# A Strassen-form MLP down projection with its matmul operands exchanged, on one core

## The chip, the core and the metric

The kernel runs on one core of one Trainium2 chip. TensorE (PE) multiplies: a stationary operand of 128x128 is loaded (PEld), then columns of a moving operand stream past it and accumulate in PSUM. VectorE (DVE) and ScalarE (ACT) work element by element, GpSimd (POOL) issues a few DMAs here, and SyncE (SP) issues most of them. The metric is the device time of one execution in microseconds, lower is better.

## The reference, cut to what matters

One layer: an input projection into two recurrent mixers, an output projection, cross attention, an MLP with squared ReLU, and a last RMSNorm. There are 512 tokens, a model width D of 2048 and a hidden width of 8192, all float32.

```python
h += concat[GDN(y_gdn), RWKV7(y_rwkv)] @ W_out
h += CrossAttn(RMSNorm(h), RMSNorm(mem))
h += SquaredReLU-MLP(RMSNorm(h))      # up: (512 x 2048) @ (2048 x 8192), square(relu), down: @ (8192 x 2048)
out = RMSNorm_final(h)
```

## The kernel before

Every product is taken in float32 precision out of float32r pieces: split() (lines 128 to 135) makes a rounded hi of a tile on ScalarE and the rest lo on VectorE, and TensorE accumulates hi·hi, hi·lo and lo·hi. Weights come through a ring of raw tiles ("ua", three buffers, and "ub", four; raw(), line 1435, loads issued by SP) and are split into rings of two ("whi", "wlo").

Up and down are each done by a Strassen form with seven products over 2x2 blocks instead of eight. In up, strassen(p) makes the hidden activations in 32 steps p of 20.16 us: seven products B11, T1, T2, B21, T3, B22, T4 (in p = 0 B21 comes second) of 24 matmuls each, with sums of weight blocks on VectorE, then the combinations of the outputs that down needs, stored to DRAM (Cd) through ScalarE's DMA queue. The product T1 of p = 0 is followed by the norm of the MLP's input: a matmul "pss", then rsq() (two ScalarE operations, lines 125 and 126), whose result is first used after product B22.

Down has four blocks c of the hidden width (2048 each). piece_() loads one combination of Cd (through SP) and splits it into activation tiles "dh" and "dl"; the list todo holds the pieces in order, and later(n) makes the next n. In a block there are seven products: 0 (weight block A11), 1 (A12), then a middle loop with 2 (S1), 3 (S1 + A11) and 4 (that + A12), then 5 (S3) and 6 (A22). The sums S1 and S3 of weight blocks are formed ahead of time by POOL: a DMA writes a block to DRAM (SUMS, "ws") and a second one adds another block to it; 18 such pairs are issued in the output projection, and 14 more by ticks in up (odd p). Each call of down() takes 1024 rows of weights by 128 output features: block() splits the tile and runs 16 matmuls with hi and 8 with lo, weights stationary, 256 tokens moving. Two calls share a PSUM bank of 128 features x 2x256 tokens, and into() adds a finished bank to the residual "hq", which lies by features (partition = feature). In the last block final() squares the results, norm() sums the squares over partitions with a matmul of ones ("pss"), and scaled() multiplies by gain and norm and stores the output by features; the half HB is finished during product 6, the half HA at the very end.

From the input projection to its end a planner in the kernel writes the order out by hand. From the output projection on, including up and down, the framework's scheduler orders each engine's instructions by their place in the program and by when it expects their data; each queue then runs in that fixed order. The tiles' semaphores follow from the data.

Of the kernel before, what the change touches and what calls it, by code (L numbers as in the profile page):

```python
# [9 lines left out]
F32 = mybir.dt.float32  # L10
# [26 lines left out]
for _n, _w in (("norm_mix", 16), ("norm_xattn", 16), ("norm_mem", 16), ("norm_mlp", 16),  # L37
               ("norm_final", 16), ("mu", 27), ("w0", 8), ("a0", 8), ("kk", 8), ("ka", 8),
               ("rk", 8), ("lnw", 8), ("lnb", 8), ("conv", 96), ("gnw", 1), ("dtb", 1),
               ("alog", 1)):  # L40
    PRM[_n] = (_off, _w)
    _off += _w
# [31 lines left out]
def build(tc, I, out):  # L74
# [268 lines left out]

    SUMS = {i: [pd.tile([P, 2048], F32, name=f"ws{i}_{u}", tag=f"ws{i}_{u}") for u in range(16)] for i in (0, 1)}
    Cd = [pd.tile([P, 7, 512], F32, name=f"cd{q}", tag=f"cd{q}") for q in range(16)]
# [953 lines left out]
    tock = pc.tile([P, 1], F32, name="tock")  # L1299
    wanted = [(i, c * 4 + u) for c in range(4) for i in (0, 1) for u in range(4)]  # L1300

    def background(h, n):

        tc.keep_in_program_order(GP.tensor_copy(tock, h[:, 0:1]))
        for _ in range(n):
            i, u = wanted.pop(0)
            tc.keep_in_program_order(GP.dma_start(SUMS[i][u], I["w_dn"][u, (2, 0)[i]]))
            tc.keep_in_program_order(GP.dma_start(SUMS[i][u], I["w_dn"][u, 1], accum_op=ALU.add, max_dma_last_dim=2048))

# [10 lines left out]
    for n in range(KD):  # L1320
        xr = sl2()
        nc.sync.dma_start(xr, I["xT"][:, n, :])
        pt = psb(f"op{n}", "mm", 2)
        gemm(pt, I["w_out"][n], KD, oh, ol)
        V.tensor_tensor(out=hres[n], in0=pt, in1=xr, op=ALU.add)
        hi, lo = act_tile(f"hh{n}"), act_tile(f"hl{n}")
        split(hres[n], hi, lo, col("norm_xattn", n))
        hh_.append(hi)
        hl_.append(lo)
        finish(n, acc)  # L1330
        if n == 0:
            background(hres[n], 18)
    pcol = psb("pcol")
# [76 lines left out]
    def add(o, a, b):  # L1410
        V.tensor_tensor(out=o, in0=a, in1=b, op=ALU.add)
# [38 lines left out]
    def strassen(p, done, used):  # L1450
# [46 lines left out]
        sub(t4, c2[:, HA], t[:, HB])  # L1497
        if p % 2 and p > 1 and wanted:
            S.copy(ticks[:, p:p + 1], c2[:, 0:1])
            background(ticks[:, p:p + 1], 1)  # L1500
# [47 lines left out]

    todo = []

    for p in range(32):
# [4 lines left out]
        def used(i):  # L1556
            if p == 0 and i == T1:
                pt = psb("pss2", "scr", 1)
                mm(pt, ones, acc)
                rsq(rstd, pt, 1.0 / 2048, b_eps6)  # L1560
            if p == 31 and i in (T1, T2, T3):
                for q in ((0,), (1, 2), (3,))[i - T1]:
                    piece_(0, 0, q)

        strassen(p, square, used)

    def later(n):
# [3 lines left out]

    EV, OD = 0, 1
    view = lambda t: t.rearrange("p (a b) -> p a b", b=M)

    def into(a, par, half, pt, op):
        h = hq[a][par][:, :, half]
        V.tensor_tensor(out=h, in0=h, in1=view(pt), op=op)

    def weights(c, m, b):
        u = c * 4 + m // 2  # L1580
        src = SUMS[b - 4][u] if b >= 4 else I["w_dn"][u, b]
        return src[:, m % 2 * 1024:m % 2 * 1024 + 1024]

    A11, A21, A22, A12, S1, S3 = range(6)

    def down(c, i, m, pt, a, start):
        parts = []
        for k in range(8):
            hi, lo = had[c, i][k // 2]
            s_ = slice(k % 2 * M, k % 2 * M + M)  # L1590
            parts.append((hi[:, s_], lo[:, s_]))
        block(pt[:, m % 2 * M:m % 2 * M + M], a, parts, start and m % 2 == 0)

    TAGS = (("mg", 2), ("mg", 2), ("scr", 1), ("scg", 1))
    sums = {}

    def final(a, par, half):

        sq = sl2()
        S.activation(view(sq), hq[a][par][:, :, half], AF.Square)  # L1600
        nm = "A" if half is HA else "B"
        if nm not in sums:
            sums[nm] = (ph if half is HB else pu).tile([P, T], F32, tag="acc" if half is HB else "ur", name=f"fs{nm}", bufs=1)
            V.tensor_copy(sums[nm], sq)
        elif (a, par, nm) == (3, OD, "A"):
            sums["last"] = sq
        else:
            add(sums[nm], sums[nm], sq)

    def norm(half, parts):  # L1610
        pt = psb("pss3", "mg")[:, HA]
        parts = [x[:, y] for x in parts for y in (HA, HB)]
        for j, x in enumerate(parts):
            mm(pt, ones, x, start=j == 0, stop=j == len(parts) - 1)
        rsq(rstd[:, half], pt, 1.0 / 2048, b_eps6)

    def scaled(n, half):
        h = hres[n][:, half]
        V.scalar_tensor_tensor(out=h, in0=h, scalar=col("norm_final", n), in1=rstd[:, half],
                               op0=ALU.mult, op1=ALU.mult)  # L1620
        (nc.sync if n % 2 else nc.scalar).dma_start(out[n][:, half], h)

    todo += [(0, i, q) for i in range(1, 7) for q in range(4)]
    SUB, ADD = ALU.subtract, ALU.add
    for c in range(4):
        end = c == 3
        nx = lambda *l: [(c + 1, i, q) for i in l for q in range(4)] if not end else []
        X = [psb(f"dx{c}_{a}", ("mx", "mm")[a // 2]) for a in range(4)]
        for m in range(8):
            down(c, 0, m, X[m // 2], raw(weights(c, m, A11)), True)  # L1630
            if m % 2:
                into(m // 2, EV, HA, X[m // 2], SUB)
            later(1)
        todo += nx(0)
        for m in range(8):
            if m % 2 == 0:
                z = psb(f"dz{c}_{m}", *TAGS[m // 2])
            down(c, 1, m, z, raw(weights(c, m, A12)), True)
            if m % 2:
                into(m // 2, EV, HA, z, ADD)  # L1640
                if end:
                    final(m // 2, EV, HA)
            later(1)
        todo += nx(1)
        for a in range(4):
            y = psb(f"dy{c}_{a}", *TAGS[a])
            ms = (2 * a, 2 * a + 1)
            s1 = [raw(weights(c, m, S1)) for m in ms]
            for m in ms:
                down(c, 2, m, y, s1[m % 2], True)  # L1650
            into(a, OD, HB, y, ADD)
            a11 = [raw(weights(c, m, A11)) for m in ms]
            for m in ms:
                add(s1[m % 2], s1[m % 2], a11[m % 2])
                down(c, 3, m, X[a], s1[m % 2], False)
            into(a, EV, HB, X[a], SUB)
            a12 = [raw(weights(c, m, A12)) for m in ms]
            for m in ms:
                add(a12[m % 2], a12[m % 2], s1[m % 2])
                down(c, 4, m, y, a12[m % 2], False)  # L1660
            into(a, EV, HB, y, SUB)
            if end:
                final(a, EV, HB)
            later(2 if c == 0 else 1)
        todo += nx(2, 3, 4)
        for m in range(8):
            down(c, 5, m, X[m // 2], raw(weights(c, m, S3)), False)
            if m % 2:
                into(m // 2, OD, HB, X[m // 2], ADD)
                if end:  # L1670
                    final(m // 2, OD, HB)
            later(1)
        todo += nx(5)
        for m in range(8):
            down(c, 6, m, X[m // 2], raw(weights(c, m, A22)), False)
            if m % 2:
                into(m // 2, OD, HA, X[m // 2], ADD)
                if end:
                    final(m // 2, OD, HA)
            later(1)  # L1680
            if end and m == 0:
                norm(HB, [sums["B"]])
                S.activation(rcol[:, 0:1], rstd[:, HB][:, 0:1], AF.Ln)
            elif end:
                for n in range((m - 1) * 16 // 7, m * 16 // 7):
                    scaled(n, HB)
        todo += nx(6)
    norm(HA, [sums["A"], sums["last"]])
    for n in range(KD):
        scaled(n, HA)  # L1690
    pu_cm.__exit__(None, None, None)
# [3 lines left out]
def layout(inputs):  # L1695
# [33 lines left out]
    for n in ("norm_mix", "norm_xattn", "norm_mem", "norm_mlp"):  # L1729
        put(n, cols(a[n][0]))  # L1730
    put("norm_final", cols(a["norm_final"]))
    mu = a["rwkv_mu"][0]
# [37 lines left out]
    d["w_up"] = blocks7(a["mlp_w_up"][0])  # L1770
    wd = blocks7(a["mlp_w_down"][0]).reshape(4, 2, 4, P, 4, 1024)
    d["w_dn"] = np.ascontiguousarray(wd.transpose(4, 0, 2, 3, 1, 5).reshape(16, 4, P, 2048))
    return d
# [16 lines left out]
```

## Time and profile before

| | |
|---|---|
| median of 3 runs | 3021.33 us (3020.08 to 3025.76) |
| the profiled execution | 3018.6 us, span 3016.8 us |
| TensorE, weight loads | busy 99% and 89% of the span |
| VectorE, ScalarE, POOL | 69%, 49%, 9% |
| chain that ended last | 92% TensorE |
| stages on TensorE | output projection from 1331, attention from 1505, up from about 1689, down from 2348 to 3002 |

Times in the profile are microseconds from the start of the span. A row of a group gives the line, the engine, the operation, the output and inputs with their shapes, how many there were, the sum of their times and the mean in ns, and the idle time before them. Matmuls overlap each other, so the spacing of their starts, not their mean length, is what a stream of them costs. A row of the order of time gives the start, the length and the number of instructions merged.

### The profile page before, as it was taken

Reading aid. Unit: us, or ns where it says so; the run is one execution under the profiler, and the core shown is the slowest. Engines: PE = TensorE matmul, PEld = TensorE weight load, DVE = VectorE, ACT = ScalarE, POOL = GpSimd, SP = SyncE. Lnnn points to the kernel's source line nnn. Section 1 sums busy time; section 2 is a strip of 40 time slices with the busy share of each in tenths; the row PEclk is TensorE's granted clock in tenths of the full one; section 3 lists DMA queues with packets and bytes.
Section 4 is the critical chain, followed back from the end, with each engine's and each line's share of the span. In section 5 each row is a group of like instructions: output and inputs, shape, how many; then the busy total and the mean of one; then the engine's idle time right before and its main releaser. Section 6 shows DMA issues by size and latency. Waiting matters only on the chain.

```text
span 3016.8 us, 56151 instructions
## 1 busy us (share of the span) xinstructions
PE 2972.4 (99%) x22912; PEld 2672.2 (89%) x22912; DVE 2077.9 (69%) x2925; ACT 1484.6 (49%) x2014; POOL 271.8 (9%) x626
## 2 busy tenths in 40 slices
PE   9999999999999999999999999999999999999998
PEld 7788878878877898878887899999999999999998
DVE  7666666666677646544437788888887886868676
ACT  6454545544556555543325544444444544444444
POOL 0302212213213000001110000000000000000000
PEclk9999999999999999999999999999999999999999
DMA  5323423323425487789994367677677877676654
GB/s 185 102 88 81 108 72 90 101 81 89 129 70 161 149 267 244 247 260 273 261 237 128 119 187 200 194 204 199 196 206 207 274 248 233 214 251 203 235 182 154
DMA packets 284626, 537.70 MB, mean 178 GB/s; under 512 B 95752, under 2 KB 148236, under 8 KB 283856
## 3 DMA queue, kind: packets, MB, share of 16 engines
q1 hardware_dynamic: 228816, 427.15, 45.7%
q0 software_dynamic: 17920, 67.11, 9.8%
q10 hardware_dynamic: 37632, 39.86, 3.7%
q8 instruction: 179, 2.93, 0.4%
q14 instruction: 79, 0.65, 0.1%
HBM read 473.86 MB, written 127.28 MB: 199 GB/s over the span
## 4 chain that ended last, share of the span: by engine, by line
PE 92%; DMA 2%; DVE 2%; ACT 2%; issue 1%; POOL 0%; ACTq 0%; SPq 0%; DVEq 0%; POOLq 0%
PE py L247 21%; PE upx L1445 8%; PE dx L1445 7%; PE op L122 6%; PE dx L1448 4%; PE upy L1445 4%; PE upx L1448 4%; PE dy L1445 4%; PE kq L247 3%; PE vo L122 3%; PE vp L122 3%; PE sc L122 3%; PE at L122 3%; PE kp L247 2%; PE dz L1445 2%; PE upy L1448 2%
## 5 line engine op out<-in xcount | busy, mean ns | idle before, releaser
L130 ACT CAST whi<-ub 128x1024 fp32r<-128x1024 f32 x259 | 271.1, 1048 | 289.5 <-PE dx L1445 73.7
L131 DVE TENSOR_TENSOR wlo<-ub,whi 128x1024 fp32r<-128x1024 f32 x259 | 316.1, 1221 | 90.9 <-ACT whi L130 90.3
L247 PE MATMUL py<-xhi,whi 128*128 128x512 f32 x928 | 371.5, 400 | 6.6 <-ACT xhi L247 6.6
L247 PE MATMUL py<-xhi,wlo 128*128 128x512 f32 x928 | 371.9, 401 | 0.0
L247 PE MATMUL py<-xlo,whi 128*128 128x512 f32 x928 | 371.4, 400 | 0.0
L247 DVE TENSOR_TENSOR wlo<-wraw,whi 128x1024 fp32r<-128x1024 f32 (+1 forms) x180 | 223.4, 1241 | 128.1 <-ACT whi L247 124.2
L130 ACT CAST whi<-ua 128x1024 fp32r<-128x1024 f32 x189 | 198.0, 1048 | 213.0 <-PE dx L1445 54.4
L247 ACT CAST whi<-wraw 128x1024 fp32r<-128x1024 f32 (+1 forms) x180 | 188.1, 1045 | 203.3 <-PE py L247 162.0
L1445 PE MATMUL upx<-cb,whi 128*128 128x256 f32 x2048 | 268.6, 284 | 4.8 <-ACT whi L130 4.5
L131 DVE TENSOR_TENSOR wlo<-ua,whi 128x1024 fp32r<-128x1024 f32 x189 | 230.7, 1221 | 58.3 <-ACT whi L130 56.5
L1445 PEld LDWEIGHTS upx<-cb,whi 128*128 128x128 f32 x2048 | 256.5, 193 | 5.7 <-ACT whi L130 5.4
L1445 PE MATMUL dx<-dh,whi 128*128 128x256 f32 x1024 | 252.1, 284 | 4.3 <-ACT whi L130 4.3
L1445 PE MATMUL dx<-dl,whi 128*128 128x256 f32 x1024 | 251.2, 283 | 0.0
L131 DVE TENSOR_TENSOR wlo<-wraw,whi 128x1024 fp32r<-128x1024 f32 x112 | 137.2, 1225 | 114.3 <-ACT whi L130 112.8
L247 PEld LDWEIGHTS py<-xhi,whi 128*128 128x128 f32 x928 | 175.0, 189 | 41.0 <-ACT xhi L247 6.6
L247 PEld LDWEIGHTS py<-xhi,wlo 128*128 128x128 f32 x928 | 175.0, 189 | 35.2 <-issue 1.0
L247 PEld LDWEIGHTS py<-xlo,whi 128*128 128x128 f32 x928 | 174.9, 188 | 35.0 <-DVE xlo L247 0.7
L1445 PEld LDWEIGHTS dx<-dh,whi 128*128 128x128 f32 x1024 | 196.5, 192 | 5.7 <-ACT whi L130 5.7
L1445 PEld LDWEIGHTS dx<-dl,whi 128*128 128x128 f32 x1024 | 196.5, 192 | 0.0
L130 ACT CAST whi<-wraw 128x1024 fp32r<-128x1024 f32 x112 | 117.8, 1052 | 155.9 <-PE op L122 68.9
L1448 PE MATMUL upx<-cb,wlo 128*128 128x256 f32 x1024 | 144.1, 283 | 0.0
L1448 PE MATMUL dx<-dh,wlo 128*128 128x256 f32 x1024 | 143.8, 283 | 0.1
(784 smaller groups left out, 6973.3 us busy)
## 6 DMA issues: line engine op xcount, KB each, us to landing
wraw<-in_w_in SPq DMA_DIRECT2D x116, 512.0 KB, 3.9
ub<-in_w_dn SPq DMA_DIRECT2D x88, 512.0 KB, 4.8
ua<-in_w_dn SPq DMA_DIRECT2D x72, 512.0 KB, 4.5
ub<-in_w_up SPq DMA_DIRECT2D x71, 512.0 KB, 4.7
ws<-in_w_dn POOLq DMA_DIRECT2D x32, 1024.0 KB, 11.9
ua<-in_w_up SPq DMA_DIRECT2D x57, 512.0 KB, 5.2
sl<-cd SPq DMA_DIRECT2D x104, 256.0 KB, 4.7
ub<-ws SPq DMA_DIRECT2D x40, 512.0 KB, 4.6
```

Of the source, the lines that this page charges most:

```text
L122: PE.matmul(o, l, r, start=start, stop=stop)
L130: S.copy(hi, src)
L131: V.tensor_tensor(out=lo, in0=src, in1=hi.bitcast(F32), op=ALU.subtract)
L247: f(*a, **k)
L1445: PE.matmul(pt, hi[:, k * P:k * P + P], x, start=start, stop=False, skip_group_check=True)
L1448: PE.matmul(pt, lo[:, k * P:k * P + P], parts[k][0], start=False, stop=k == 7, skip_group_check=True)
```

## The change

In down(), the operands change places. A call now takes 256 rows of the contraction (one piece q) by 512 output features: the activations are stationary, 128 tokens at a time, and 512 weight columns move. A call runs 12 matmuls instead of 24, and there are as many calls. Results lie by tokens, so the residual is needed by tokens too: turn() transposes it on TensorE in up (p = 2 to 17) and stores it to DRAM (HTd), held() loads it back into the same SBUF as "G" (p = 20 to 27). The squares of the last norm are summed along the row by ScalarE (accum_out), the gain is loaded as four broadcast rows, and the output is stored by tokens. The weights are laid out anew on the host. SUMS has 64 tiles of half the size, 36 pairs in the output projection and one at each p from 2 to 29. The norm of up follows T3 instead of T1. The middle loop holds four s1 tiles (in "ub") and goes through products 2, 3 and 4 with four calls each, for two halves m of the output.

```diff
-    wanted = [(i, c * 4 + u) for c in range(4) for i in (0, 1) for u in range(4)]
+    wanted = [(i, c * 8 + u) for c in range(4) for i in (0, 1) for u in range(8)]
...
-            background(hres[n], 18)
+            background(hres[n], 36)
...
-        if p % 2 and p > 1 and wanted:
+        if p > 1 and wanted:
             S.copy(ticks[:, p:p + 1], c2[:, 0:1])
             background(ticks[:, p:p + 1], 1)
...
+    def turn(a, t):
+        pt = psb(f"ht{a}_{t}", ("scr", "scg")[t % 2], 1)
+        for j in range(4):
+            PE.transpose(pt[:, j * P:(j + 1) * P], hres[4 * a + j][:, t * P:(t + 1) * P], ident)
+        r = (ph if t % 2 else pu).tile([P, T], F32, tag=("ur", "acc")[t % 2], name=f"hr{a}_{t}", bufs=1)
+        S.copy(r, pt)
+        nc.sync.dma_start(HTd[:, t, a * 512:a * 512 + 512], r)
+
+    def held(t, m):
+        i = t * 2 + m
+        G[t][m] = ph.tile([P, 2, T], F32, tag=f"h{i // 2}{i % 2}", name=f"g{t}{m}", bufs=1)
+        nc.sync.dma_start(G[t][m], HTd[:, t, m * 1024:m * 1024 + 1024].rearrange("p (a b) -> p a b", b=T))
...
-            if p == 0 and i == T1:
+            if p == 0 and i == T3:
                 pt = psb("pss2", "scr", 1)
                 mm(pt, ones, acc)
                 rsq(rstd, pt, 1.0 / 2048, b_eps6)
...
         strassen(p, square, used)
+        if 2 <= p < 18:
+            turn((p - 2) // 4, (p - 2) % 4)
+        elif 20 <= p < 28:
+            held((p - 20) // 2, p % 2)
...
+    def into(half, blk, m, pts, op):
+        for t in (0, 1):
+            g = G[2 * half + t][m][:, blk, :]
+            V.tensor_tensor(out=g, in0=g, in1=pts[t], op=op)
...
+    def down(c, i, q, pts, a, start):
+        cnt[0] += 1
+        hi = pw.tile([P, 1024], F32R, tag="whi", name=f"whi{cnt[0]}", bufs=NWS)
+        lo = pw.tile([P, 1024], F32R, tag="wlo", name=f"wlo{cnt[0]}", bufs=NWS)
+        split(a, hi, lo)
+        uh, ul = had[c, i][q]
+        st = [(z, t, slice(z * M + t * P, z * M + t * P + P), slice(z * 512, z * 512 + 512)) for z in (0, 1) for t in (0, 1)]
+        for z, t, x, w in st:
+            PE.matmul(pts[t], uh[:, x], hi[:, w], start=start and z == 0 and q == 0, stop=False, skip_group_check=True)
+            PE.matmul(pts[t], ul[:, x], hi[:, w], start=False, stop=False, skip_group_check=True)
+        for z, t, x, w in st:
+            PE.matmul(pts[t], uh[:, x], lo[:, w], start=False, stop=z == 1 and q == 3, skip_group_check=True)
...
+    def final(half, blk, m):
+        for t in (2 * half, 2 * half + 1):
+            i = t * 4 + m * 2 + blk
+            S.activation(sl2(), G[t][m][:, blk, :], AF.Square, accum_out=ss[:, i:i + 1])
+
+    def norm(half):
+        h = slice(2 * half, 2 * half + 2)
+        V.tensor_reduce(out=rt[:, h], in_=ss[:, half * 8:half * 8 + 8].rearrange("p (a b) -> p a b", b=4), axis=AX.X, op=ALU.add)
+        rsq(rt[:, h], rt[:, h], 1.0 / 2048, b_eps6)
+
+    def scaled(t, n):
+        g = G[t][n // 2][:, n % 2, :]
+        V.scalar_tensor_tensor(out=g, in0=g, scalar=rt[:, t:t + 1], in1=gain[n], op0=ALU.mult, op1=ALU.mult)
+        (nc.sync if n % 2 else nc.scalar).dma_start(out[t][:, n * 512:n * 512 + 512], g)
...
+        for m in (0, 1):
+            y = [psb(f"dy{c}_{m}{t}", *TAGS[m][t]) for t in (0, 1)]
+            s1 = []
+            for q in range(4):
+                u = (c * 2 + m) * 4 + q
+                s1.append(raw(SUMS[0][u], 0))
+                down(c, 2, q, y, s1[q], True)
+            into(1, 1, m, y, ADD)
+            for q in range(4):
+                a = raw(I["w_dn"][(c * 2 + m) * 4 + q, A11], 1)
+                add(s1[q], s1[q], a)
+                down(c, 3, q, X[m], s1[q], False)
+            into(1, 0, m, X[m], SUB)
+            for q in range(4):
+                a = raw(I["w_dn"][(c * 2 + m) * 4 + q, A12], 1)
+                add(a, a, s1[q])
+                down(c, 4, q, y, a, False)
+                if c == 0 and q % 2:
+                    later(1)
+            into(1, 0, m, y, SUB)
...
+    norm(0)
+    for n in range(4):
+        for t in (0, 1):
+            scaled(t, n)
```

More of the change, by code (lines that the diff above doesn't have):

```diff
@@ L37 @@
 for _n, _w in (("norm_mix", 16), ("norm_xattn", 16), ("norm_mem", 16), ("norm_mlp", 16),
-               ("norm_final", 16), ("mu", 27), ("w0", 8), ("a0", 8), ("kk", 8), ("ka", 8),
+               ("mu", 27), ("w0", 8), ("a0", 8), ("kk", 8), ("ka", 8),
                ("rk", 8), ("lnw", 8), ("lnb", 8), ("conv", 96), ("gnw", 1), ("dtb", 1),
@@ L342, in build @@
     VOd = [pd.tile([P, 8, 512], F32, name=f"vod{i}", tag=f"vod{i}") for i in range(4)]
-    SUMS = {i: [pd.tile([P, 2048], F32, name=f"ws{i}_{u}", tag=f"ws{i}_{u}") for u in range(16)] for i in (0, 1)}
+    SUMS = {i: [pd.tile([P, 1024], F32, name=f"ws{i}_{u}", tag=f"ws{i}_{u}") for u in range(32)] for i in (0, 1)}
+    HTd = pd.tile([P, 4, 2048], F32, name="htd", tag="htd")
     Cd = [pd.tile([P, 7, 512], F32, name=f"cd{q}", tag=f"cd{q}") for q in range(16)]
@@ L1307, in background @@
             tc.keep_in_program_order(GP.dma_start(SUMS[i][u], I["w_dn"][u, (2, 0)[i]]))
-            tc.keep_in_program_order(GP.dma_start(SUMS[i][u], I["w_dn"][u, 1], accum_op=ALU.add, max_dma_last_dim=2048))
+            tc.keep_in_program_order(GP.dma_start(SUMS[i][u], I["w_dn"][u, 1], accum_op=ALU.add, max_dma_last_dim=1024))
     def finish(n, acc):
@@ L1549, in build @@
     todo = []
+    G = [[None] * 2 for _ in range(4)]
+    def turn(a, t):
[9 more added lines that the diff above has]
+        nc.sync.dma_start(G[t][m], HTd[:, t, m * 1024:m * 1024 + 1024].rearrange("p (a b) -> p a b", b=T))
     for p in range(32):
@@ L1570, in later @@
                 piece_(*todo.pop(0))
[L1572 to L1582, printed above, removed]
-    A11, A21, A22, A12, S1, S3 = range(6)
[L1586 to L1621, printed above, removed]
+    A11, A21, A22, A12, S1, S3 = range(6)
@@ new lines, in build, with weights @@
+    SUB, ADD = ALU.subtract, ALU.add
+    TAGS = ((("mg", 2), ("mg", 2)), (("scr", 1), ("scg", 1)))
+    def weights(c, m, q, b):
+        u = (c * 2 + m) * 4 + q
+        return raw(SUMS[b - 4][u] if b >= 4 else I["w_dn"][u, b])
+    def into(half, blk, m, pts, op):
[14 more added lines that the diff above has]
+            PE.matmul(pts[t], uh[:, x], lo[:, w], start=False, stop=z == 1 and q == 3, skip_group_check=True)
@@ new lines, in build @@
+    ss = pc.tile([P, 16], F32, name="ss")
+    rt = pc.tile([P, 4], F32, name="rt")
+    gain = []
+    def final(half, blk, m):
[6 more added lines that the diff above has]
+        rsq(rt[:, h], rt[:, h], 1.0 / 2048, b_eps6)
@@ L1623, in build @@
+    def scaled(t, n):
+        g = G[t][n // 2][:, n % 2, :]
+        V.scalar_tensor_tensor(out=g, in0=g, scalar=rt[:, t:t + 1], in1=gain[n], op0=ALU.mult, op1=ALU.mult)
+        (nc.sync if n % 2 else nc.scalar).dma_start(out[t][:, n * 512:n * 512 + 512], g)
     todo += [(0, i, q) for i in range(1, 7) for q in range(4)]
-    SUB, ADD = ALU.subtract, ALU.add
+    both = [(m, q) for m in (0, 1) for q in range(4)]
     for c in range(4):
@@ L1627, in build @@
         nx = lambda *l: [(c + 1, i, q) for i in l for q in range(4)] if not end else []
[L1628 to L1632, printed above, removed]
+        X = [[psb(f"dx{c}_{m}{t}", ("mx", "mm")[m]) for t in (0, 1)] for m in (0, 1)]
+        for m, q in both:
+            down(c, 0, q, X[m], weights(c, m, q, A11), True)
+            if q == 3:
+                into(0, 0, m, X[m], SUB)
@@ L1633, in build @@
             later(1)
         todo += nx(0)
[L1635 to L1640, printed above, removed]
+        for m, q in both:
+            if q == 0:
+                z = [psb(f"dz{c}_{m}{t}", *TAGS[m][t]) for t in (0, 1)]
+            down(c, 1, q, z, weights(c, m, q, A12), True)
+            if q == 3:
+                into(0, 0, m, z, ADD)
@@ L1641, in build @@
                 if end:
-                    final(m // 2, EV, HA)
+                    final(0, 0, m)
             later(1)
         todo += nx(1)
[L1645 to L1661, printed above, removed]
+        for m in (0, 1):
+            y = [psb(f"dy{c}_{m}{t}", *TAGS[m][t]) for t in (0, 1)]
+            s1 = []
+            for q in range(4):
+                u = (c * 2 + m) * 4 + q
+                s1.append(raw(SUMS[0][u], 0))
[13 more added lines that the diff above has]
+            into(1, 0, m, y, SUB)
@@ L1662, in build @@
             if end:
-                final(a, EV, HB)
-            later(2 if c == 0 else 1)
+                final(1, 0, m)
         todo += nx(2, 3, 4)
[L1666 to L1669, printed above, removed]
+        if end:
+            for n in range(4):
+                g = (ph if n == 1 else pu).tile([P, T], F32, tag=("ur", "acc", "tt", "tt")[n], name=f"gain{n}", bufs=(1, 1, 2, 2)[n])
+                nc.sync.dma_start(g, I["nf"][:, n * 512:n * 512 + 512].broadcast_to([P, 512]))
+                gain.append(g)
@@ L1670, in build @@
+        for m, q in both:
+            down(c, 5, q, X[m], weights(c, m, q, S3), False)
+            if q == 3:
+                into(1, 1, m, X[m], ADD)
                 if end:
-                    final(m // 2, OD, HB)
+                    final(1, 1, m)
             later(1)
         todo += nx(5)
[L1674 to L1677, printed above, removed]
+        for m, q in both:
+            down(c, 6, q, X[m], weights(c, m, q, A22), False)
+            if q == 3:
+                into(0, 1, m, X[m], ADD)
@@ L1678, in build @@
                 if end:
-                    final(m // 2, OD, HA)
+                    final(0, 1, m)
             later(1)
[L1681 to L1686, printed above, removed]
+            if end and (m, q) == (0, 0):
+                norm(1)
+                S.activation(rcol[:, 0:1], rt[:, 2:3], AF.Ln)
+            elif end and (m, q) != (1, 3):
+                for _ in range(1 if m == 0 and q < 3 else 2):
+                    if done:
+                        scaled(*done.pop(0))
@@ L1687, in build @@
+            if end and (m, q) == (0, 0):
+                done = [(t, n) for n in range(4) for t in (2, 3)]
         todo += nx(6)
-    norm(HA, [sums["A"], sums["last"]])
-    for n in range(KD):
-        scaled(n, HA)
+    norm(0)
+    for n in range(4):
+        for t in (0, 1):
+            scaled(t, n)
     pu_cm.__exit__(None, None, None)
@@ L1730, in layout @@
         put(n, cols(a[n][0]))
-    put("norm_final", cols(a["norm_final"]))
     mu = a["rwkv_mu"][0]
@@ L1770, in layout @@
     d["w_up"] = blocks7(a["mlp_w_up"][0])
-    wd = blocks7(a["mlp_w_down"][0]).reshape(4, 2, 4, P, 4, 1024)
-    d["w_dn"] = np.ascontiguousarray(wd.transpose(4, 0, 2, 3, 1, 5).reshape(16, 4, P, 2048))
+    wd = a["mlp_w_down"][0].reshape(4, 4, 2, 2, P, 2, 2, 512)
+    wd = np.stack([wd[:, :, :, k, :, :, n] for n, k in ((0, 0), (1, 0), (1, 1), (0, 1))])
+    d["w_dn"] = np.ascontiguousarray(wd.transpose(1, 5, 2, 0, 4, 3, 6).reshape(32, 4, P, 1024))
+    d["nf"] = np.ascontiguousarray(a["norm_final"].reshape(1, 2048))
     return d
@@ L1783 @@
            for n, v in arrays.items()}
-    out = nc.dram_tensor("out_0_dram", (16, P, T), F32, kind="ExternalOutput").ap()
+    out = nc.dram_tensor("out_0_dram", (4, P, 2048), F32, kind="ExternalOutput").ap()
     with tile.TileContext(nc) as tc:
@@ L1788 @@
     y = np.asarray(r.results[0]["out_0_dram"])
-    return np.ascontiguousarray(y.reshape(2048, T).T).reshape(1, T, 2048)
+    return np.ascontiguousarray(y.reshape(1, T, 2048))
```

## The prediction

> **What bounds the kernel now.** I read the page's busy shares first, then the table of stages for the stretches that the change touches, then the order of time on TensorE inside them, and last the waits of the queues.
>
> ```profile
> PE 2972.4 (99%) x22912; PEld 2672.2 (89%) x22912; DVE 2077.9 (69%) x2925; ACT 1484.6 (49%) x2014; POOL 271.8 (9%) x626
> ```
> ```profile
> core 0: us, PE busy (x) PEld busy (x) DVE busy (x) ACT busy (x) POOL busy (x), PEclk, DMA share, GB/s
> 1690.00:1716.65 26.65, 22.53 (x162) 21.39 (x162) 20.32 (x27) 14.59 (x22) 0.00 (x0) 0.87 0.36 118
> 2348.39:2400.00 51.61, 48.24 (x395) 47.40 (x394) 38.54 (x50) 29.36 (x41) 0.00 (x0) 1.00 0.87 288
> 2400.00:3002.19 602.19, 600.61 (x4990) 599.27 (x4989) 454.35 (x492) 277.40 (x313) 0.00 (x0) 1.00 0.66 217
> 3002.19:3016.80 14.61, 1.98 (x8) 1.07 (x7) 7.11 (x17) 2.80 (x4) 0.00 (x0) 0.69 0.42 144
> ```
> Down runs from 2348.39 to 3002.19, 653.8 us. TensorE is busy for 600.61 of the last 602.19 us, at full granted clock, while VectorE has 75%, ScalarE 46% and the DMA engines 66%. So down is a stream of matmuls, and its price is their number times their spacing.
>
> **The change: the matmuls of down.** The lo products (line 1448) are a third of down's matmuls, and the trace groups them:
>
> ```profile
> L1448 PE MATMUL dx<-dh,wlo 128*128 128x256 f32 x1024 | 143.8, 283 | 0.1
> L1448 PE MATMUL dy<-dh,wlo 128*128 128x256 f32 x512 | 72.0, 283 | 0.0
> L1448 PE MATMUL dz<-dh,wlo 128*128 128x256 f32 x256 | 35.9, 283 | 0.0
> ```
> That is 1792, so 5376 in all (4 blocks x 7 products x 8 half tiles x 24), each over 256 columns. Afterwards there are 4 x 7 x 8 calls of down() with 12 matmuls of 512 columns: 2688. Columns and products stay; the instructions and their weight loads are halved. Spacing, not the modelled mean of 283 ns, is what counts, and a dense stretch gives it:
>
> ```profile
> 2480.00:2650.00 170.00, 170.00 (x1417) 169.82 (x1416) 127.60 (x136) 80.00 (x91) 0.00 (x0) 1.00 0.71 232
> ```
> ```profile
> 1331.13:1505.21 174.08, 174.08 (x769) 144.14 (x769) 67.93 (x76) 51.56 (x64) 17.67 (x24) 1.00 0.93 262
> ```
> ```profile
> 1544.71 0.39 PE L122 MATMUL sc<-kqh,hl 128*128 128x512 f32 x1
> 1544.93 0.39 PE L122 MATMUL sc<-kqh,hh 128*128 128x512 f32 x1
> ```
> 170.00/1417 is 120.0 ns for 256 columns. The output projection, 512 columns throughout, takes 174.08 us for its 768 matmuls (the window's count has one of a neighbour): 226.7 ns. The score matmuls "sc" already have the new arrangement (activations stationary, freshly split weights moving, 512 wide), and start 0.22 to 0.23 us apart. So 2 x 120.0 - 226.7 = 13.3 ns go for each pair, a fixed part per instruction. Down's stream is 5376 x 120.0 = 645.1 us now (653.8 less idle time, restarts and a norm) and 2688 x 226.7 = 609.4 after: **-35.7 us**.
>
> A rule of the Trainium skill speaks against this. "TensorE: Matmul & The Clock Gate", section "Back-to-back issue gap", gives the isolated warm spacing as N/2.4 + 2.5 ns; by it the halving would save 2688 x 2.5 = 6.7 us, and the sum below would end at -4 instead of -33. The rows above differ: 120.0 and 226.7 ns lie on a line with a fixed part of 13.3 ns, and the measurement decides.
>
> **The residual, transposed in up.** turn() adds four 128x128 transposes in each of 16 products. The attention probabilities show their price among float32r matmuls:
>
> ```profile
> 1607.03 0.48 PE L122 MATMUL at<-plo,whi 128*128 128x512 f32 x1
> 1607.35 0.60 PE L1383 MATMUL ptr<-cst,pr 128*128 128x128 f32 x4
> 1607.70 0.48 PE L122 MATMUL at<-phi,wlo 128*128 128x512 f32 x1
> 1608.02 0.40 PE L122 MATMUL at<-phi,whi 128*128 128x512 f32 x1
> ```
> Four take 1607.35 to 1607.70, and the matmul behind them 0.32 instead of 0.23: 0.35 + 0.09 = 0.44 us, x16 = **+7.0 us**, all on TensorE's path. The lower end is 16 x 0.35 = 5.6; the upper is 64 separate interruptions at 0.09 + 0.09, 11.5.
>
> The same page, "Part 4: PE-mode transpose", reports about 275 ns for a transpose in a kernel's context. As a spacing that would be 64 x 0.275 = 17.6 us and the sum 10.6 us worse; the trace has four in 0.35 us.
>
> Beside it ScalarE gets 16 evacuations and 14 more ticks, VectorE nothing, SP 16 stores of 256 KB and 8 loads of 512 KB (held()).
>
> ```profile
> 1740.00:2320.00 580.00, 575.84 (x4793) 575.15 (x4793) 475.33 (x570) 278.54 (x385) 27.16 (x42) 1.00 0.70 200
> ```
> ```profile
> L1499 ACT COPY ticks<-sl 128x1 f32<-128x1 f32 x14 | 2.7, 192 | 0.4
> ```
> An evacuation is at most one cast of twice its width (1048 ns, below): under 17 us plus 2.7 us in a stage where ScalarE is idle for 301 of 580 us; without that cover it costs all 20. The 8.4 MB more are 14 GB/s beside 200. Taken at nothing. The stores, though, wait on SP for fresh data, which in mid up only two piece loads do today; behind each stand the weight loads of the next product. What such a wait costs is shown once:
>
> ```profile
> SPq L1543 <- DMA cd<-sl: 12.9, 2, 7.9
> ```
> ```profile
> 1745.87 0.33 SPq L1543 DMA_DIRECT2D cr<-cd  x1
> 1789.14 0.33 SPq L1543 DMA_DIRECT2D cr<-cd  x1
> ```
> ```profile
> 1745.45 2.08 PE L1445 MATMUL upz<-cb,whi 128*128 128x256 f32 x16
> 1765.61 2.08 PE L1445 MATMUL upz<-cb,whi 128*128 128x256 f32 x16
> 1785.77 2.08 PE L1445 MATMUL upz<-cb,whi 128*128 128x256 f32 x16
> 1805.93 2.08 PE L1445 MATMUL upz<-cb,whi 128*128 128x256 f32 x16
> ```
> The two loads held SP for 12.9 us together, 7.9 in one, and up's products still followed at their 20.16 us without a loss. I take **+1 us**; the ends are 0 and +10 (0.6 us at each of 16).
>
> **The norm of up moved from T1 to T3.**
>
> ```profile
> 1695.81 1.28 ACT L125 ACT_TABLE_LOAD   x1
> 1697.10 0.69 ACT L125 ACTIVATE rstd<-pss,cb_e 128x512 f32<-128x512 f32 x1
> 1697.81 1.28 ACT L126 ACT_TABLE_LOAD   x1
> 1699.10 0.63 ACT L126 ACTIVATE rstd<-rstd 128x512 f32<-128x512 f32 x1
> 1699.64 0.39 ACT L130 CAST cb<-sl 128x256 fp32r<-128x256 f32 x1
> ```
> ```profile
> 1702.75 3.78 PE L1445 MATMUL upx<-cb,whi 128*128 128x256 f32 x16 [3.43 <-ACT whi L130]
> ```
> Today rsq() holds ScalarE for 3.9 us ahead of a cast of comb; VectorE's adds and the cast of T2's weights come after it, TensorE idles 3.43 us, and the next 16 matmuls take 3.78 instead of 2.08 us (that stretch has a granted clock of 0.87). At T3 two products are split ahead, 5.8 us of cover for 3.9, and comb is done. 3.4 + 1.7 could go; I take **-4**, ends -7 (with the smaller gaps of that stretch) and +2 (the same holding ScalarE when the first store of p = 0 is due).
>
> **The new order inside down.** Banks of PSUM are read four calls before they are written again; VectorE's work per call is as before. What is new is how buffers are held: s1[0..3] take all four "ub" buffers for a half of the middle loop, and the loads of A11 and A12 share three "ua" buffers.
>
> ```profile
> L130 ACT CAST whi<-ub 128x1024 fp32r<-128x1024 f32 x259 | 271.1, 1048 | 289.5 <-PE dx L1445 73.7
> L131 DVE TENSOR_TENSOR wlo<-ub,whi 128x1024 fp32r<-128x1024 f32 x259 | 316.1, 1221 | 90.9 <-ACT whi L130 90.3
> ua<-in_w_dn SPq DMA_DIRECT2D x72, 512.0 KB, 4.5
> ```
> For product 4 one turn of an "ua" buffer is 4.5 (load) + 1.22 (add, as the split) + 1.05 + 1.22 = 8.0 us; three calls of 12 x 226.7 ns are 8.2. That fits only just, but product 3 releases its buffer after the add, so the first three loads are early and only the fourth call is tight. VectorE needs there, per 12 calls, 20 x 1.22 plus 6 into() of at most as much: 24.4 to 31.7 of 32.6 us. Ends: +16 (2 us at each of 8 half loops) and -4 (the first product now needs one piece per call instead of four at once, and 2348 to 2400 has 51.61 - 48.24 = 3.4 us idle). I take **+1**. POOL's 64 smaller pairs are the same bytes and run out at p = 29 as before; the last of them are for down's fourth block. They hide in POOL's idle time (27 of 580 us busy in the row of up above); with that gone, the middle loops and product 5 would wait for the sums.
>
> **The end.**
>
> ```profile
> 3001.06 1.12 PE L1448 MATMUL dx<-dh,wlo 128*128 128x256 f32 x8
> 3002.02 1.02 PE L122 MATMUL pss<-fsA,cst 128*128 128x256 f32 x4
> 3002.22 0.69 DVE L1577 TENSOR_TENSOR h<-h,dx 128x512 f32<-128x512 f32 x1 [1.62 <-PE dx L1448]
> ...
> 3007.02 6.42 DVE L1619 SCALAR_TENSOR_TENSOR h<-h,prm,rstd 128x256 f32<-128x256 f32 x16 [4.12 <-ACT rstd L126]
> ```
> Squares are summed by ScalarE along tokens' rows, so the first half's pss matmuls (1.0 us, as the group shown) leave TensorE. From the last matmul to the first scaled() it is 4.8 us now; afterwards two into() and two squares instead of one, no matmul, and an rsq() of two columns: 1.3 + 0.7 + 0.2 + 1.28 (table) + 0.4, with the steps between an estimated 4.3. Then 8 of 512 columns instead of 16 of 256: at the 0.60 us that a 0.69 us operation occupies, 4.8 instead of 6.4; the last store is twice as large. Together **-2**, ends -5 and +2 (2 MB of output at the 262 GB/s quoted above need 8 us, whoever computes faster).
>
> **Sum.** -35.7 + 7.0 + 1 - 4 + 1 - 2 = -32.7 us. The profiled execution took 3018.6 us (span 3016.8), the median of the runs is 3021.3, 2.7 higher; so 2986 beside that execution and **2988 us** beside the median.
>
> **The rivals.**
> *No fixed part to save.* Did the 13.3 ns belong to the columns, 512 would cost 240 ns, the first term vanish and the rest give +3: 3024 us. By the rule of the Trainium skill cited above it would be 3018. Against it stand the two spacings and the "sc" rows. 4 in 100.
> *Buffers bound the middle loop.* The turn of 8.0 us against 8.2 speaks for it, the early loads against. At 2 to 2.5 us in each of 8 half loops, +16 to +20 instead of +1: 3003 to 3008 us. 11 in 100.
> *Slower, by SP's order.* If the stores stand ahead of loads that could run a product earlier, the first weights of the next product land 4.5 us after the store and are cast 1.05 later: 5 us idle at each of 16 products, +80 instead of +1, 3067 us. It decides from 2.1 us a product on (34/16), and passes 0.2% from 2.5. For it: SP issues in order, and up reuses seven buffers. Against it: the 7.9 us wait above that cost nothing. 7 in 100.
> The forecast has 78 in 100, its own range 2975 to 3003: below, all lower ends together (-46); above, the two that are likeliest to fall together, transposes and SP (+13.5). With the second rival taken in, 2975 to 3008. A measurement of this kernel can tell some 0.2% (6 us) from no change: faster 0.89 (forecast and second rival), the same 0.05, slower 0.06.
>
> **What would show it.** The table of stages should give 2688 matmuls of 512 columns in down, some 227 ns apart, and down about 618 us long; up's products 20.6 us apart from p = 2 to 17 and 20.16 after; no 3.4 us gap at T2 of p = 0, and ScalarE's table loads behind T3. Wrong, if TensorE idles for "ua" loads in the middle of each block, if SP's waits name the transposed tile with TensorE's gaps behind them, or if the spacing of the 512-wide matmuls is over 235 ns.

## The result, and the profile after

The changed kernel takes 2991.37 us (median, 2985.1 to 2993.6) beside 3021.33 before: a ratio on record of 0.9893, 95% interval 0.9878 to 0.9908 (the two medians alone give 0.9901). A second measurement, beside other experiments, gave 2989.09 and 0.9901 (0.9884 to 0.9917). The profiled execution took 2992.58 us, with a span of 2990.5, 26.3 less than before's 3016.8.

First the table of stages of the changed kernel, with the same columns as before. The rows are up's first step p = 0, three stretches of down, and the end; the number behind the last bracket is the granted clock.

```profile
1692.51:1718.91 26.40, 24.33 (x189) 22.53 (x188) 21.11 (x28) 17.79 (x27) 0.00 (x0) 1.00 0.50 160
2356.64:2400.00 43.36, 40.17 (x169) 32.27 (x168) 32.00 (x41) 24.00 (x33) 0.00 (x0) 0.96 0.89 303
2400.00:2480.00 80.00, 78.37 (x335) 61.73 (x334) 71.97 (x80) 40.58 (x50) 0.00 (x0) 1.00 0.77 256
2480.00:2650.00 170.00, 170.00 (x750) 140.40 (x750) 134.64 (x147) 85.80 (x101) 0.00 (x0) 1.00 0.75 251
2976.90:2990.50 13.60, 0.18 (x1) 0.00 (x0) 6.83 (x11) 3.16 (x7) 0.00 (x0) 0.67 0.45 154
```
The fourth row answers to the dense stretch before: 170.00 us for 750 matmuls, 226.7 ns each, where the old kernel had 1417 of 120.0 ns. In it weight loads are shown for 140.40 us, not for all 170. The second and third rows hold 504 matmuls in 123.4 us, where 114.3 would do: 9 us are lost at the start of down and almost none later. The last third of down's matmuls, the lo products, are now these groups:

```profile
L1616 PE MATMUL dx<-wlo,dh 128*128 128x512 f32 x512 | 138.5, 392 | 0.6 <-DVE wlo L131 0.6
L1616 PE MATMUL dy<-wlo,dh 128*128 128x512 f32 x256 | 68.9, 391 | 0.8 <-DVE wlo L131 0.8
L1616 PE MATMUL dz<-wlo,dh 128*128 128x512 f32 x128 | 34.2, 389 | 0.0
```
That is 896, a third of 2688. (The modelled mean rose from 283 to 391 ns; it says nothing of the spacing.)

Stages in us, by the starts of their first matmuls; down ends with the start of its last. "Up, rest" is up without p = 0.

| kernel | start of up | up, p = 0 | up, rest | down | end |
|---|---|---|---|---|---|
| before | 1688.7 | 27.9 | 631.7 | 653.5 | 14.9 |
| after | 1692.5 | 26.4 | 637.7 | 620.0 | 13.8 |
| after, second profile | 1688.5 | 26.4 | 637.0 | 619.7 | 13.8 |

Down gives 33.5 us and the end 1.1. Up takes 4 back. The start of up, 3.8 us later in the first profile after, lies in stages that the change does not touch, and the second profile does not have it.

### The profile page after: what moved, and what is told of

It is laid out like the page before. It is cut to its first block, busy times and chain, and to the rows that moved or that the text cites. A ratio compares the mean times of both kernels' runs of the same rounds, so it can differ in the third digit from the quotient of the medians.

```text
span 2990.5 us, 51003 instructions
## 1 busy us (share of the span) xinstructions
PE 2948.0 (99%) x20276; PEld 2537.2 (85%) x20276; DVE 2064.4 (69%) x2896; ACT 1491.7 (50%) x2060; POOL 324.8 (11%) x704
## 4 chain that ended last, share of the span: by engine, by line
PE 89%; DMA 4%; DVE 3%; ACT 2%; issue 1%; POOL 0%; ACTq 0%; SPq 0%; DVEq 0%; POOLq 0%
PE py L247 21%; PE upx L1446 7%; PE op L122 6%; PE upy L1446 4%; PE upx L1449 4%; PE dx L1613 3%; PE dx L1614 3%; PE dx L1616 3%; PE sc L122 3%; PE kq L247 3%; PE kp L247 3%; PE at L122 3%; PE vo L122 3%; PE upz L1446 2%; PE upy L1449 2%; PE vp L122 2%
## 5 line engine op out<-in xcount | busy, mean ns | idle before, releaser
L130 ACT CAST whi<-ub 128x1024 fp32r<-128x1024 f32 x267 | 280.1, 1051 | 284.1 <-PE dx L1614 67.8
L131 DVE TENSOR_TENSOR wlo<-ub,whi 128x1024 fp32r<-128x1024 f32 x267 | 325.6, 1222 | 111.5 <-ACT whi L130 108.5
L130 ACT CAST whi<-ua 128x1024 fp32r<-128x1024 f32 x181 | 190.2, 1051 | 204.9 <-PE dx L1614 58.0
L131 DVE TENSOR_TENSOR wlo<-ua,whi 128x1024 fp32r<-128x1024 f32 x181 | 221.1, 1222 | 64.2 <-ACT whi L130 63.7
L1613 PE MATMUL dx<-whi,dh 128*128 128x512 f32 x512 | 200.1, 391 | 3.7 <-ACT whi L130 2.9
L1614 PE MATMUL dx<-whi,dl 128*128 128x512 f32 x512 | 199.6, 390 | 0.0
L1616 PE MATMUL dx<-wlo,dh 128*128 128x512 f32 x512 | 138.5, 392 | 0.6 <-DVE wlo L131 0.6
L1446 PE MATMUL upy<-cb,whi 128*128 128x256 f32 x1024 | 134.0, 283 | 0.0
L1449 PEld LDWEIGHTS upx<-cb,wlo 128*128 128x128 f32 x1024 | 132.1, 192 | 0.0
```

What stands on the lines that cost most here:

```text
L130: S.copy(hi, src)
L131: V.tensor_tensor(out=lo, in0=src, in1=hi.bitcast(F32), op=ALU.subtract)
L1446: PE.matmul(pt, hi[:, k * P:k * P + P], x, start=start, stop=False, skip_group_check=True)
L1449: PE.matmul(pt, lo[:, k * P:k * P + P], parts[k][0], start=False, stop=k == 7, skip_group_check=True)
L1613: PE.matmul(pts[t], uh[:, x], hi[:, w], start=start and z == 0 and q == 0, stop=False, skip_group_check=True)
L1614: PE.matmul(pts[t], ul[:, x], hi[:, w], start=False, stop=False, skip_group_check=True)
```

## The experiments

My theory after the result: the saving is the fixed part of a matmul instruction, halved in number; up pays for the transposes; nothing else matters. The rivals: that the exchanged operands or down's new order saved the time; that the moved norm, the halved sums or SP's stores in up count too.

**The width alone.**

```diff
-            PE.matmul(pts[t], uh[:, x], hi[:, w], ...)
+            for b in range(2):    # 256 columns each; likewise ul·hi and uh·lo
+                PE.matmul(pts[t][:, b * 256:b * 256 + 256], uh[:, x], hi[:, v], ...)
```


> The changed kernel with each 512-column matmul of down() given as two of 256 columns; operands, layout, buffers and everything else stay as changed. If the saving is a fixed 13.3 ns per matmul instruction, down (first dx to last dx, 620.3 us in the profile after) takes 620.3 + 2688 x 13.3 ns = 656 us and the kernel 3027 us, 0.2% above the kernel before. If the saving came from the exchanged operands or from the new order of down itself, down stays near 620 us and the kernel near 2991.

The time is 3017.83 us, ratio 0.9994 (0.9983 to 1.0005). Down takes 653.7 us, as before the change. The table of stages in the stretch that was quoted for both kernels:

```profile
2480.00:2650.00 170.00, 170.00 (x1419) 170.00 (x1418) 125.14 (x135) 77.86 (x89) 0.00 (x0) 1.00 0.71 232
```
That is 119.8 ns again. The width of the moving operand carries the whole gain in down; exchanged operands and the new order by themselves are worth nothing. (The total came out 9 us under the forecast of 3027, which had started from the slower profiled execution: up, whose code is that of the changed kernel, took 659.3 us here, beside 664.1 and 663.4 in the two profiles after. That difference matters further down.)

**A quarter of the width.** The same edit with four matmuls of 128 columns.

> The changed kernel with each 512-column matmul of down() given as four of 128 columns. If the spacing is columns/2.4 ns plus a fixed 13.3 ns, it is 66.7 ns and down takes 4 x 2688 x 66.7 ns = 717 us and some 11 lost, 728. If a weight load sets a floor that 256 columns just hide (spacing 120 ns), or float32r needs more passes below 256 columns, down takes 1290 us or more.

A single execution: 4662.02 us, down 2291.9. The line that I had put through two widths does not go on to a third:

```profile
2700.00:3600.00 900.00, 900.00 (x4221) 900.00 (x4220) 184.89 (x196) 115.42 (x134) 0.00 (x0) 0.50 0.20 66
```
The spacing is 900/4221 = 213.2 ns, and the granted clock (after the last x) is 0.50, without a gap on TensorE. So the two measured widths are a fact for 256 and 512 columns and no law. Whether the weight load, a slower mode of float32r or, in part, the halved clock sets the 213 ns, one execution can't say.

**No transposes.**

```diff
-        PE.transpose(...) x4;  S.copy(r, pt);  nc.sync.dma_start(HTd[:, t, a * 512:a * 512 + 512], r)
+        nc.sync.dma_start(HTd[:, t, a * 512:a * 512 + 512], hres[4 * a + t])
```


> The changed kernel without the 64 transposes and their 16 evacuations; the residual goes to DRAM as it lies (16 stores of the same size on SP, the same 8 loads), so the output is not the layer's. My reading of the profile after: 18 of the 64 transposes lie in the first product step of up, where TensorE waits anyway, and the other 46 cost 0.11 us each: up falls from 664.1 to about 659 us. If all 64 cost it falls by 7.0, to 657. If it is SP's stores that cost up its time, up stays near 664.

This kernel leaves the transposes out, so its output is not the layer's; it serves for the time alone. 2987.94 us, 0.990 (0.9887 to 0.9914), between the two ratios of the changed kernel (0.9893 and 0.9901): no gain that can be told from noise. Up's rest falls to 631.5 us, but p = 0 rises to 28.3. The price of a turn is plain in the changed kernel, in the starts of three successive B21 products in the order of time:

```profile
1849.55 2.08 PE L1446 MATMUL upz<-cb,whi 128*128 128x256 f32 x16
1870.13 2.08 PE L1446 MATMUL upz<-cb,whi 128*128 128x256 f32 x16
1890.72 2.08 PE L1446 MATMUL upz<-cb,whi 128*128 128x256 f32 x16
```
20.58 and 20.59 instead of 20.16: 0.43 us, of which 0.36 stand at the transposes. And p = 0 shows where a part of them costs nothing. First TensorE in the changed kernel, then the table's row of the kernel before:

```profile
1698.26 1.02 PE L122 MATMUL pss<-acc,cst 128*128 128x512 f32 x2
1698.71 2.47 PE L1446 MATMUL upy<-cb,whi 128*128 128x256 f32 x16
1701.61 0.87 PE L1557 MATMUL ht<-cst,h 128*128 128x128 f32 x6 [0.42 <-ACT rstd L125]
1704.33 1.42 PE L1557 MATMUL ht<-cst,h 128*128 128x128 f32 x8 [0.67 <-ACT hr L1559]
1706.52 2.17 PE L1446 MATMUL upx<-cb,whi 128*128 128x256 f32 x16 [0.77 <-ACT whi L130]
```
```profile
1688.75:1716.65 27.90, 23.78 (x172) 22.64 (x171) 21.20 (x28) 15.84 (x23) 0.00 (x0) 0.88 0.36 114
```
The scheduler had pulled 18 of the 64 transposes, which are ready early, into p = 0, 16 of them between T1 (upy) and T2 (upx). From T1 to T2 it is 7.81 us here, and 7.80 in the kernel before (1694.95 to 1702.75), where TensorE idled for 3.43 us at one go. So these 16 cost nothing. With them no gap is over 0.8 us, the granted clock of p = 0 is 1.00 instead of 0.88, T2's 16 matmuls take 2.17 us instead of 3.78, and p = 0 is 1.5 us shorter.

The kernel without transposes has one gap of 4.86 us and a clock of 0.88:

```profile
1703.15 3.78 PE L1446 MATMUL upy<-cb,whi 128*128 128x256 f32 x16 [4.86 <-ACT whi L130]
```
```profile
1691.52:1719.86 28.34, 23.30 (x172) 22.27 (x170) 21.57 (x28) 15.96 (x23) 0.00 (x0) 0.88 0.59 206
```
But that gap stands ahead of T1, not T2: the scheduler also placed rsq() with its table loads (from 1698.24 on) ahead of the cast of T1's weights (1702.07), which in the changed kernel comes before them (1697.57 and 1699.57). So its p = 0, 1.9 us longer, differs in more than the transposes.

**The place of the norm.** `if p == 0 and i == T1:` instead of T3, and, the other way, the matmul "pss" pinned:

> The changed kernel with the norm of up written after T1 again, as before. If the scheduler places it by readiness, TensorE's order and p = 0 (26.4 us) stay as they are, and up at 664 us within 1. If the move to T3 did something, p = 0 gets 2 to 4 us longer.

```diff
-                mm(pt, ones, acc)
+                tc.keep_in_program_order(PE.matmul(pt, ones, acc, start=True, stop=True))
```


> The changed kernel with the matmul of up's norm pinned behind T3's matmuls in TensorE's order (in the changed kernel it runs ahead of T1, though it is written after T3). If rsq() holding ScalarE ahead of comb's last cast makes the gap in p = 0, that step falls from 26.4 us to about 22 to 23 and up from 664 to about 660 us. If the gap comes from the adds and casts of the weights alone, p = 0 stays at 26 us, and up at 664.

With T1 written again, TensorE's order is the same instruction for instruction and p = 0 takes 26.5 us (a single execution, 2983.73 us; up 658.8). In the rows above "pss" at 1698.26 stands ahead of T1's first matmul (upy, 1698.71), though the program has it after T3: this edit of the change does nothing. Pinned, the norm does leave the way: p = 0 falls to 24.9 us, not to the 22 to 23 hoped for, since TensorE still waits 1.46 us for the cast of T2's weights and 0.79 us for VectorE's part of T1's. Only 4 transposes lie there now, and the kernel stays at 2990.42 us, 0.9907 (0.9894 to 0.9921).

**The sums alone,** in the kernel before (halved tiles, 36 pairs at first, one at each p).

> The kernel before with the one part of the change that halves the sum transfers: 64 pairs of 512 KB instead of 32 of 1 MB, 36 in the output projection and one at each p from 2 to 29. They hide in POOL's idle time: 3019 us, within 3 us of before. If the larger number of POOL DMAs disturbs the weight loads of the output projection or of up, 5 to 10 us slower; if the larger bursts did, as much faster.

3012.54 us, 0.998 (0.9969 to 0.999): 6 us faster, and not the nothing that I expected. Down is unchanged at 653.1 us; up's rest falls from 631.7 to 626.6 us. TensorE's idle time there is 1.1 us:

```profile
1716.00:2342.00 626.00, 624.89 (x5205) 624.48 (x5205) 518.04 (x623) 307.54 (x438) 62.64 (x84) 1.00 0.73 201
```
So up has gaps that come and go. Was it the even spread?

**The sums by twos,** in the changed kernel: two copies, then two additions, 18 times at first and at odd p.

> The changed kernel with its sums issued two at a time again, both copies and then both additions (18 times in the output projection, at odd p in up), the same bytes in the same 512 KB transfers. If the even spread of the sums is what made the kernel before 6 us faster in the run with halved sums, this gives it back: 5 to 6 us slower than the changed kernel, up 5 us longer. If the gain came from the size of the transfers alone, no change.

2984.18 us, 0.9879 (0.9864 to 0.9894): 5 us under the changed kernel beside it instead of slower. Up's rest is 630.1 us. That fells "even spread"; and the size alone is not it either, for the changed kernel has the halved size and the gaps. (Whether twos are really faster is open: the single execution of the kernel with T1, 2983.73 us, lies among these runs.)

**Stores of the residual on ScalarE's queue,** with the loads of "G".

> The changed kernel with the 16 stores of the transposed residual and its 8 loads issued by ScalarE's queue instead of SP's. In the profile after, SP waits 60 us in total at those stores, and up has 3 to 8 us of gaps beside the transposes against 1.5 in the kernel before with halved sums. If the gaps come from weight loads held up behind the stores on SP, up gets 2 to 6 us shorter (655 to 657) and the kernel about 2985. If they come from the additional traffic or from ScalarE's waits for slots of 'sl', up stays at 659 to 664 or gets longer by the issues on ScalarE (24 x 0.37 us).

2995.55 us, 0.9917 (0.9902 to 0.9931); up 668.8 us, 5 to 6 longer. Taking the stores off SP gains nothing. SP does wait at them in the changed kernel (the waits of SP, up):

```profile
SPq L1560 <- ACT hr L1559: 48.0, 13, 7.7
```
48 us, up to 7.7 each, but TensorE's waits in the middle of up (4.7 us) are all for ScalarE's casts, and none of those casts was late for a weight load. More issues on ScalarE, however, do harm, and that pointed to what happens ahead of a gap. This is ScalarE, and then TensorE, in the second profile of the changed kernel:

```profile
1903.09 3.07 ACTq L1506 DMA_DIRECT2D cd<-tt  x1
1906.26 1.90 ACTq L1507 DMA_DIRECT2D cd<-t  x1
1908.27 0.37 ACT L1476 COPY sl<-upy 128x256 f32<-128x256 f32 x1 [4.93 <-DMA cd<-sl]
1908.54 1.99 ACT L130 CAST whi<-ub 128x1024 fp32r<-128x1024 f32 x2
```
```profile
1909.64 2.18 PE L1446 MATMUL upz<-cb,whi 128*128 128x256 f32 x16 [2.09 <-ACT whi L130]
```
The rows with ACTq are DMA issues. Two stores of up take 3.07 and 1.90 us to issue; the cast for the next product waits behind them in ScalarE's order, and TensorE waits 2.09 us. (The tag at the copy names a DMA; the time before it is the two issues.) Not every gap is of this kind. The largest in the first profile of the changed kernel has short issues ahead of it:

```profile
2071.70 0.37 ACTq L1504 DMA_DIRECT2D cd<-sl  x1
2073.84 1.04 ACTq L1507 DMA_DIRECT2D cd<-t  x1
2078.77 0.37 ACT L1476 COPY sl<-upy 128x256 f32<-128x256 f32 x1 [5.09 <-DMA cd<-sl]
```
```profile
2080.14 3.51 PE L1446 MATMUL upz<-cb,whi 128*128 128x256 f32 x16 [2.06 <-ACT whi L130]
```
From 2074.9 to 2078.7 ScalarE waits for a store that it issued at 2071.70 to land, 7.0 us later, because the copy writes into one of the three "sl" buffers that the store reads. Here the tag is right, and the cost is a buffer, not an issue.

The issue of "tt" over the whole of up, shortest, median and longest in ns, for before, after, after again, the halved sums alone, and the sums by twos:

```profile
L1505 ACTq DMA_DIRECT2D cd<-tt x32: 366/427/4342, 1721.1 to 2355.5; - x32
```
```profile
L1506 ACTq DMA_DIRECT2D cd<-tt x32: 366/427/2690, 1723.4 to 2361.5; - x32
```
```profile
L1506 ACTq DMA_DIRECT2D cd<-tt x32: 366/427/3807, 1719.3 to 2356.6; - x32
```
```profile
L1506 ACTq DMA_DIRECT2D cd<-tt x32: 366/427/1153, 1720.5 to 2350.2; - x32
```
```profile
L1508 ACTq DMA_DIRECT2D cd<-tt x32: 366/427/1279, 1722.3 to 2352.5; - x32
```
The three with gaps have issues of 2.7 to 4.3 us, the two without none over 1.3. But the longest issue does not say how long TensorE waits in all. The kernel with the norm at T1 again and the one with 256 columns, whose code in up is the changed kernel's, have issues of 2.8 and 2.7 us and yet these waits of TensorE:

```profile
PE upz L1446 <- ACT whi L130: 1.7, 2, 1.0
```
```profile
PE upz L1446 <- ACT whi L130: 1.3, 2, 0.8
```
Only an edit can tell cause from companion:

**The stores of "tt" and "t4" off ScalarE,** in the changed kernel, to SP and to POOL.

```diff
-        nc.scalar.dma_start(Cd[p // 2][:, 4:6, h], v(t))
-        nc.scalar.dma_start(Cd[p // 2][:, 6, h], t4)
+        nc.sync.dma_start(Cd[p // 2][:, 4:6, h], v(t))       # the other kernel: nc.gpsimd
+        nc.sync.dma_start(Cd[p // 2][:, 6, h], t4)
```


> The changed kernel with up's stores of 'tt' and 't4' (the third and fourth of a step) issued by SP instead of ScalarE. In the profiles so far a gap in up follows where ScalarE takes 2.5 to 4.3 us to issue the store of 'tt' instead of 0.4 (before, after, and four variants); in the two kernels without gaps (the one before with halved sums, and the one with sums by twos) no issue takes over 1.6 us. If the issue is what holds up the casts behind it, up's rest after its first step falls from 637 to about 631 us and the kernel from 2989 to about 2984. If SP's fixed order takes its place (weight loads behind stores that wait for VectorE), up stays or gets longer. If the gaps have another cause and the slow issue is a companion, it stays at 637.

> The same two stores issued by POOL, behind its sums. If ScalarE's slow issue makes the gaps, up's rest falls from 637 to about 631 us and the kernel from 2989 to about 2984, unless a store behind a sum that waits up to 8 us for its first transfer holds the two buffers of 'tt' too long: then VectorE waits and up gets longer. If the slow issue is a companion only, 637.

SP: 2981.61 us, 0.987 (0.9854 to 0.9885). POOL: 2982.62 us, 0.9873 (0.9856 to 0.989). These are 6 to 10 us under the two medians of the changed kernel, and all their runs (2980.2 to 2983.9) lie under all nine of its (2985.1 to 2993.9). Up takes 658.0 and 656.4 us. TensorE's waits in up, in the changed kernel's second profile and then with SP:

```profile
PE upz L1446 <- ACT whi L130: 5.5, 4, 2.1
```
```profile
PE upx L1449 <- DVE wlo L131: 1.1, 2, 0.8
```
The waits for ScalarE's casts are gone; with POOL none are left at all. The slow issue itself moved along (on SP "t4" takes up to 4.1 us), and costs little there. The two versions have the lowest medians of this study and can't be told apart.

How much the stores cost is less sure than that. In the changed kernel's code, up took 664.1, 663.4, 661.3, 660.3, 659.3 and 658.8 us in six kernels' profiles (the changed kernel twice, the ones with 128 and 256 columns, with the pieces' loads on POOL and with T1), with TensorE waiting 4.7, 5.5, 3.5, 2.7, 1.3 and 1.7 us for ScalarE's casts. Moving the stores removes these waits, and both profiles lie below all six; but the gain in up is anything from 1 to 8 us, by the execution compared. The kernel with T1 orders TensorE's instructions as the changed one does, and its 2983.73 us lie among SP's runs. Of SP's gain, 3 us lie in down (617.2 us); why stays open.

**The start of down.** Piece loads on POOL instead of SP:

> The changed kernel with the loads of down's pieces (all but the first four) issued by POOL, which is idle in down, instead of SP. In the changed kernel the first 124 us of down hold 504 matmuls, which at 226.7 ns would take 114.3: 9 us are lost there and almost nothing later. If they are lost because piece loads stand behind weight loads that wait for buffers in SP's fixed order, down falls from 620 to about 614 us and the kernel by some 5 us. If the DMA engines themselves are full there (303 GB/s in the first 43 us), down stays at 620 or gets longer.

2996.02 us, 0.9918 (0.9901 to 0.9935): slower, down 631.5 us. In the stretch that should have gained, 308 matmuls fit instead of 335, and ScalarE still waits for the pieces, as its row of that stretch shows:

```profile
2400.00:2480.00 80.00, 71.42 (x308) 57.28 (x308) 68.66 (x76) 39.16 (x48) 10.72 (x20) 1.00 0.72 236
```
```profile
ACT dh L130 <- DMA sl<-cd: 13.6, 5, 4.7
```
POOL itself waits at these loads (2350 to 2480: 48.4 us at 16 loads; up to 14.9, for buffers that VectorE still reads). What would win back the 9 us stays open.

## Why the prediction was right, point by point

The direction, the time (2988 against 2991 and 2989) and the range held. Of the terms of the sum, one carries the result and held; of the small ones several were wrong and cancelled. The terms in up add to +4 (7.0 + 1 - 4), and up took 3.8 to 4.5 us more in the two profiles. That is luck: the norm's -4 did not come by its move, 16 transposes were free, and up itself changes by 5 us between executions of the same code, with gaps that the sum did not have. (The upper end of the range adds up to 3002, not 3003.)

- **The matmuls of down, -35.7.** Right in mechanism and size: 226.7 ns by the rows after, and 119.8 ns again when only the width is taken back. Down fell by 33.5 us, because about as much as before, and 2 to 3 us more, is lost in its first block. By the rule of the Trainium skill, page "TensorE: Matmul & The Clock Gate", section "Back-to-back issue gap", the prediction estimated 6.7; the runs differ from it.
- **The transposes, +7.0.** The price of one was right (0.43 us for four). But I had put them at p = 2 to 17 because the program has them there, and 18 of 64 ran in p = 0, 16 of them in a wait where they cost nothing. The other 46 come to an estimated 4.9 us (0.107 each). Taking all of them out gains nothing that can be told from noise.
- **The norm at T3, -4.** The step that failed. It rested on the place in the program; the scheduler places the matmul by readiness, and it runs ahead of T1 either way. ScalarE's table loads still stand ahead of T2 (1699.57 and 1701.57), not behind T3. The time from T1 to T2 stayed at 7.8 us; of the loss that I saw there (3.4 us of gap, 1.7 of a lower clock) only the second went, 1.6 us at T2, now that transposes fill the gap.
- **The sums, at nothing.** Mis-sized: halving them is worth 6 us in the kernel before, and ScalarE's slow issues are gone with it (none of "tt" over 1.2 us); that they are the way was not tested there. In the changed kernel the slow issues are back and the gain is not seen.
- **SP's stores, +1.** The slower rival did not come: SP waited 48 us at the stores and no wait of TensorE is traced to them. But TensorE's waits in up, 1.3 to 5.5 us in different executions, stand behind ScalarE's stores (their issue, and once a buffer that a store held), which I had not looked at: the prediction's table of instructions counts DMA issues as not busy, and I let 49% busy stand for a free engine.
- **The middle loop, +1.** Right from the second block on: the stretch from 2480 to 2650 has no idle time at 226.7 ns. The rival with the buffers did not come.
- **The end, -2.** Right: 1.1 us in the end and a norm less inside down. From the end of the last matmul, at 2977.1, to the first scaled() it is 4.0 us, where 4.3 were estimated:

```profile
2976.89 1.29 DVE L1603 TENSOR_TENSOR g<-g,dx 128x512 f32<-128x512 f32 x2 [3.53 <-PE dx L1616]
...
2981.07 5.39 DVE L1635 SCALAR_TENSOR_TENSOR g<-g,rt,gain 128x512 f32<-128x512 f32 x8 [1.88 <-ACT rt L126]
```

## What to carry to other kernels

In a dense stream of matmuls, read the spacing (stretch over count) at each width that the trace has, and turn the operands so that the wide one moves: from 256 to 512 columns this saved 13.3 ns for each pair, 33 us here; the same reordering without the width saved nothing. Where a scheduler orders the instructions, their place in the program is not their place on the engine: look up the order in the trace before a move is given a price. And read a queue's DMA issues beside an engine's busy time: an engine that is half idle can still hold up everything behind a store that takes 3 us to issue. Before a gain of some us is put down to an edit, compare several executions of the same code.

## What the runs showed of the hardware that was not expected

- The issue of the store of "tt" on ScalarE takes 0.43 us in the median, and 1.8 to 4.3 us at some steps of up; in the changed kernel's two profiles the longest issues, of "tt" or "t4", are some 144 us apart. With both on another queue, TensorE no longer waits for ScalarE's casts (1.3 to 5.5 us with them on ScalarE). What a slow issue waits for, the runs don't show.
- Float32r matmuls of 128 columns were granted a clock of 0.50 for two milliseconds without a gap, and follow each other in 213.2 ns, nearly as long as 512 columns take at 1.00 (226.7). The Trainium skill, page "TensorE: Matmul & The Clock Gate", section "Part 1: The HAM clock gate (the "warmup" mystery)", lists a half clock when idle and a full one when busy, and says that activity releases the throttle. The 0.50 agrees with the half clock; a stream without gaps that stays there does not agree with the release.
- With 16 transposes in a wait ahead of T2 the granted clock of p = 0 was 1.00, with TensorE idle there 0.88 (the kernel before), and the matmuls after the wait took 2.17 us instead of 3.78: filling a gap with work that has to be done anyway paid twice.
